# Merging three attention groups beside a triangular inverse instead of in the last stage

## The chip, the cores and the metric

The kernel runs on one core of one Trainium2 chip. The metric is the device time of one execution in microseconds (us); before the change the median of three runs is 2359.2 us. The engines are named PE (TensorE, matrix products), DVE (VectorE), ACT (ScalarE), POOL (GpSimd) and SP (SyncE, which only issues DMA transfers). Each engine works through its own instructions in a fixed order; an instruction that waits holds up all that stand behind it on that engine.

## What is computed

One decoder layer over 2048 tokens of width 1024, in float32. A normalised input is projected once; from the result two mixers run in parallel: a chunked gated delta rule (4 heads) and a dilated sliding-window attention in three groups (window 128, 512, 2048; dilation 1, 4, 16), each with 4 heads of 128. Both are gated, projected back, merged and added to the input. Cut to what matters here:

```python
tmat = triangular_solve(eye + lower, eye)           # per head and chunk of 64 tokens, 128 of them
...                                                 # the scan over chunks uses tmat
outs, lses = [], []
for gi, (window, dilation) in enumerate(SWA_GROUPS):
    o_g, lse_g = dilated_window_attention(sq[:, :, gi], sk[:, :, gi], sv[:, :, gi], window, dilation)
    outs.append(o_g); lses.append(lse_g)
alpha = softmax(stack(lses, axis=0), axis=0)        # over the three groups
o_swa = sum(alpha[..., None] * stack(outs, axis=0), axis=0)
o_swa = o_swa * silu(swa_z)
y_swa = o_swa.reshape(B, T, SWA_WIDTH) @ w_branch_swa
...
x = x + (sigmoid(g_dn) * y_dn + sigmoid(g_swa) * y_swa) @ w_out
```

The change concerns the two lines with `alpha`, here called the merge.

## The kernel before

PE does every matrix product as three products of a high and a low part of each operand, to keep float32 precision. The program is written as a sequence of PE work with hooks: after every six large matmuls `hook` advances a counter called a tick and runs whatever was put off to that tick with `at(delay, fn)`. So the order of instructions on each engine follows from ticks. From the opening of the inverse on, the order is not pinned: a planner places each instruction as early as its inputs, its buffers and its engine allow by the planner's own times, the earlier in the program first. That is why loads often stand far ahead of their place in the program.

The stages, with the times of the profile:

1. Up to about 1000 us: input projections for the attention and, between them, the attention itself. Each attention block writes its unnormalised output (128 columns), its negated maximum and its denominator (columns 128 and 129) to a DRAM buffer `oscr` of shape [T, 3 groups, 4 heads, 130].
2. `cunits` (PE matmuls at lines 720 to 722): 36 units of four blocks, 24 matmuls of 128x512 to a block, four ticks to a block. PE's results go through three PSUM banks. The units produce the delta rule's inputs (to about 1415 us), then the gates z (`z_block`, ACT and DVE, lines 1148 and 1149) and g (`g_block`, ACT only, line 1155). Each unit's weights are loaded by SP (line 697) and split into a high part by ACT (line 87) and a low part by POOL (line 88).
3. Beside the gate units, from 1415 us: `inverse`. Z with the 128 lower triangles is loaded (2 MB, line 1003), then 63 rows follow one another on DVE: a product of i x i elements (line 1020), two memsets (1021, 1022) and a reduction (1023). Row i+1 is put off by as many ticks as the row should take. After the last row the result is stored to `vscr` and, transposed by ACT and DVE (lines 1014, 1015), to `tscr`.
4. Still beside the gate units: `scan`, 16 steps. Its loads come first (lines 1042 to 1048); its first matmul (line 1058) is put off by 26 ticks from the end of the inverse. Its results go to the DRAM buffer `odn`.
5. `start_fin`, still beside the gate units: `o_load` for the first two tiles of 128 tokens, and 12 ticks later `o_start`, which transposes the four heads of `odn` and of the merge on PE (line 1221), multiplies with z (DVE, line 1222) and splits (ACT line 1225, POOL line 1226).
6. The final stage: for each of eight blocks of 256 tokens, eight `fin_y` (branch products at lines 1237 to 1239; DVE 1241, POOL 1243, ACT 1244, POOL 1245) and four `fin_out` (products with w_out at 1254 to 1256). In the first block the weights w_out are still being loaded and split (lines 1175, 1182, 1184). Between them the next two tiles' `o_load` and `o_start`.

`o_load(t)` loads `odn` for tile t (line 1212) and calls `combine(t)`, the merge: a load of 780 KB from `oscr` (line 1189), the minimum of the negated maxima (1194), the differences and their exponentials (1195, 1196 on ACT), the weights by the denominators (1197 to 1200), three products of 128x512 (1203) and two sums (1205, 1206). All but the exponential is on DVE. The buffer `oc` of the load exists once, the result `osw` twice.

Of the kernel before, what the change touches and what calls it, by code (L numbers as in the profile page):

```python
# [47 lines left out]
class Net:  # L48
# [7 lines left out]
    def setup(self):  # L56
        tc, nc, ctx, i = self.tc, self.nc, self.ctx, self.i
        self.cp = cp = ctx.enter_context(tc.tile_pool(name="const", bufs=1))
        hp = ctx.enter_context(tc.tile_pool(name="hp", bufs=1))
        self.hh = hp.tile([P, NB, KT, 512], F32R, name="hh")  # L60
        self.hl = hp.tile([P, NB, KT, 512], F32R, name="hl")
        self.hhf = self.hh.bitcast(F32)
        self.ident = cp.tile([P, P], F32, name="ident")
        self.mhalf = cp.tile([P, 8], F32, name="mhalf")
        nc.vector.memset(self.mhalf, -0.5)
        self.ab = cp.tile([P, 8, 16], F32, name="ab")
        self.step = 0
        self.tick = 0
        self.ev = []
        self.gcscr = self.scratch("gcscr", [2 * H * T])  # L70
        self.nbscr = self.scratch("nbscr", [H * T])
        self.rec = self.scratch("rec", [16, P, H, RECW])
        self.lscr = self.scratch("lscr", [H * 32, 64, 64])
        self.vscr = self.scratch("vscr", [H * 32, 64, 64])
        self.tscr = self.scratch("tscr", [H * 32, 64, 64])
        self.odn = self.scratch("odn", [T, H * P])
        self.zscr = self.scratch("zscr", [8, P, T])
        self.gscr = self.scratch("gscr", [16, P, T])
        self.qks = [[self.scratch(f"qks{h}{g}", [T, 256]) for g in range(G)] for h in range(H)]
        self.vs = [self.scratch(f"vs{g}", [T, 512]) for g in range(G)]  # L80
        self.opd = {(p, op, x): self.scratch(f"opd{p}{op}{x}", [P, 4, 512])
                    for p, op in ((0, "A11"), (0, "A12"), (0, "A21"), (0, "A22"), (1, "A21")) for x in range(2)}
        self.wdr = [[self.scratch(f"wdr{j}{x}", [P, 1024]) for x in range(2)] for j in range(56)]
        self.oscr = self.scratch("oscr", [T, G, H, 130])

    def split(self, raw, h, l, eng):
        self.nc.scalar.activation(h, raw, AF.Copy)  # L87
# [1090 lines left out]
    def w_split(self, which, k0, m, raw):  # L1178
# [4 lines left out]
        eng = nc.gpsimd if (k0 and m % 2) else nc.vector  # L1183
        eng.tensor_tensor(out=lv, in0=raw, in1=hv.bitcast(F32), op=ALU.subtract)

    def combine(self, t):
        nc, fp, V = self.nc, self.fp, self.nc.vector
        oc = fp.tile([P, G, H, 130], F32, name="oc", bufs=1)
        nc.sync.dma_start(oc.rearrange("p g h c -> p (g h c)"), dr(self.oscr, t * P * G * H * 130, [[G * H * 130, P], [1, G * H * 130]]))
        sm = fp.tile([P, 4, 12], F32, name="cs", bufs=1)  # L1190
        nm, ls = oc[:, :, :, 128], oc[:, :, :, 129]
        mn, e, c, r = sm[:, 0, 0:4], sm[:, 1, :].rearrange("p (g h) -> p g h", h=H), \
            sm[:, 2, :].rearrange("p (g h) -> p g h", h=H), sm[:, 3, 0:4]
        V.tensor_reduce(out=mn.unsqueeze(2), in_=nm.rearrange("p g h -> p h g"), axis=mybir.AxisListType.X, op=ALU.min)
        V.tensor_tensor(out=e, in0=mn.unsqueeze(1).to_broadcast([P, G, H]), in1=nm, op=ALU.subtract)
        nc.scalar.activation(e, e, AF.Exp)
        V.tensor_tensor(out=c, in0=e, in1=ls, op=ALU.mult)
        V.tensor_reduce(out=r.unsqueeze(2), in_=c.rearrange("p g h -> p h g"), axis=mybir.AxisListType.X, op=ALU.add)
        V.reciprocal(r, r)
        V.tensor_tensor(out=c, in0=e, in1=r.unsqueeze(1).to_broadcast([P, G, H]), op=ALU.mult)  # L1200
        o = fp.tile([P, H, P], F32, name="osw", bufs=2)
        for g in range(G):
            V.tensor_tensor(out=oc[:, g, :, 0:P], in0=oc[:, g, :, 0:P], in1=c[:, g, :].unsqueeze(2).to_broadcast([P, H, P]),
                            op=ALU.mult)
        V.tensor_tensor(out=o, in0=oc[:, 0, :, 0:P], in1=oc[:, 1, :, 0:P], op=ALU.add)
        V.tensor_tensor(out=o, in0=o, in1=oc[:, 2, :, 0:P], op=ALU.add)
        return o

    def o_load(self, t, x):
        nc, fp = self.nc, self.fp  # L1210
        od = fp.tile([P, H, P], F32, name="od", bufs=2)
        nc.sync.dma_start(od.rearrange("p h c -> p (h c)"), dr(self.odn, t * P * 512, [[512, P], [1, 512]]))
        x[t] = (od, self.combine(t))

    def o_prep(self, t, b, x, oh, ol):
        nc, fp = self.nc, self.fp
# [55 lines left out]
    def run(self):  # L1272
# [50 lines left out]
        pst = ExitStack()  # L1323
        self.ps = self.ctx.enter_context(tc.tile_pool(name="ps", bufs=2, space=PSUM, **tile_))
        self.scb = 2
        cst, smst, dst, ist, qst, fst = (ExitStack() for _ in range(6))
        self.rawp = self.ctx.enter_context(tc.tile_pool(name="rawp", bufs=3, **tile_))
        sm = pool(cst, "sm")
        self.gp = pool(cst, "gp")
# [16 lines left out]
        def start_inverse():  # L1346
            self.nb_out()
            pin.close()
            dst.close()
            self.inverse(pool(ist, "ip", "right"), start_scan)  # L1350

        def start_scan():
# [30 lines left out]
        du = [partial(f, h) for h in range(H) for f in (self.k_block, self.q_block, self.v_block)]  # L1383
        self.cunits(zu[:3] + du + zu[3:] + gu, {3: open_dn, 15: lambda: self.at(9, start_inverse)}, tail)
        self.flush()
        cst.close()
        self.lp = pool(fst, "lp")
        oh, ol = xo["o0"]
# [59 lines left out]
```

## Time and profile before

| | |
|---|---|
| median of three runs | 2359.2 us (2356.81 to 2360.14) |
| profiled execution | 2357.82 us |
| its span, first to last instruction | 2356.0 us |
| mean granted TensorE clock | 0.99 |
| DMA | 263.45 MB read, 185.89 MB written |

A page of the profile gives the busy time of each engine and its share of the span. The view by stage gives, for stretches of time, how long each engine was busy; the view of waits says who waited for whom, with the total, the number of times and the longest, in us; the timeline lists single instructions with start, duration, engine, line, operation, output and inputs, and in brackets the idle time of the engine just before and what ended it. "x3" behind a row are three instructions merged into one. The groups list gives count, total busy time, and mean in ns. The list of DMA issues gives size and the time from issue to landing.

### The profile page before, as it was taken

The numbers are of one execution on the slowest core, as the hardware profiler recorded it, in microseconds if no ns is written. First come the engines' busy times: TensorE is split into PE (matmuls) and PEld (weight loads), VectorE is DVE, ScalarE is ACT, GpSimd is POOL, SyncE is SP. The second block draws the span as 40 slices with busy tenths as digits, with TensorE's granted clock in tenths as the row PEclk, the third lists the DMA queues.
The fourth block names the chain that finished last, engine by engine and source line by source line (L and its number), as shares of the span: only waits on it lengthen the run. The fifth ranks groups of instructions, "written<-read, shape, count | busy, mean of one in ns | idle before, by whom it ended". The sixth has DMA issues, their size and how long they took to land.

```text
span 2356.0 us, 43344 instructions
## 1 busy us (share of the span) xinstructions
PE 2297.1 (97%) x15216; PEld 2086.2 (89%) x15216; DVE 1347.7 (57%) x2853; ACT 907.2 (39%) x2948; POOL 889.2 (38%) x1331
## 2 busy tenths in 40 slices
PE   7999999979999999999999999999999999999999
PEld 7999999879999999888787888888888788889988
DVE  6566576594435535445777767999244423444431
ACT  5345466653324435445666651111233214111110
POOL 5374266574403303402675561111232213433442
PEclk8999999999999999999999999999999999999999
DMA  9989889857887888853544443222677636554542
GB/s 296 325 277 323 272 283 292 269 161 239 251 265 236 246 273 261 259 148 101 130 110 132 127 103 113 72 76 69 212 207 208 193 120 175 161 179 150 148 139 77
DMA packets 525969, 452.23 MB, mean 192 GB/s; under 512 B 66168, under 2 KB 490424, under 8 KB 523320
## 3 DMA queue, kind: packets, MB, share of 16 engines
q1 hardware_dynamic: 525464, 449.39, 62.6%
q8 instruction: 121, 1.98, 0.3%
q14 instruction: 96, 0.79, 0.1%
q10 hardware_dynamic: 288, 0.07, 0.0%
HBM read 263.45 MB, written 185.89 MB: 191 GB/s over the span
## 4 chain that ended last, share of the span: by engine, by line
PE 66%; DMA 5%; DVE 3%; POOL 1%; ACT 1%; issue 1%; SPq 0%; DVEq 0%; POOLq 0%; ACTq 0%
PE mm L433 12%; PE mm L720 10%; PE mm L721 10%; PE mm L722 10%; PE mm L1254 2%; PE mm L1256 2%; PE mm L1255 2%; PE mm L1237 2%; PE mm L1239 2%; PE mm L1238 2%; DMA oscr<-ol 2%; DMA gcb<-gcscr 1%; PE tp L584 1%; PE po L626 1%; DMA raw<-in_w_out_dram 1%; PE tp L617 1%
## 5 line engine op out<-in xcount | busy, mean ns | idle before, releaser
L720 PE MATMUL mm<-hh,w 128*128 128x512 f32 x1152 | 463.3, 402 | 0.0
L722 PE MATMUL mm<-hh,w 128*128 128x512 f32 x1152 | 457.8, 397 | 0.0
L721 PE MATMUL mm<-hl,w 128*128 128x512 f32 x1152 | 456.9, 397 | 0.0
L433 PE MATMUL mm<-w,hh 128*128 128x256 f32 x1760 | 328.3, 286 | 0.0
L433 PEld LDWEIGHTS mm<-w,hh 128*128 128x128 f32 x1760 | 271.2, 190 | 0.0
L88 POOL TENSOR_TENSOR w<-raw,w 128x512 fp32r<-128x512 f32 x68 | 100.0, 1472 | 435.0 <-ACT w L87 434.8
L720 PEld LDWEIGHTS mm<-hh,w 128*128 128x128 f32 x1152 | 220.3, 191 | 45.9
L722 PEld LDWEIGHTS mm<-hh,w 128*128 128x128 f32 x1152 | 217.0, 188 | 46.9
L433 PE MATMUL mm<-hh 128*128 128x256 f32 x880 | 257.5, 293 | 0.0
L721 PEld LDWEIGHTS mm<-hl,w 128*128 128x128 f32 x1152 | 217.6, 189 | 42.4
L433 PE MATMUL mm<-hl,hh 128*128 128x256 f32 x880 | 249.8, 284 | 0.9 <-POOL hl L295 0.9
L433 PE MATMUL mm<-hh,hl 128*128 128x256 f32 x880 | 249.6, 284 | 0.0
L433 PE MATMUL mm<-w,hl 128*128 128x256 f32 x880 | 248.3, 282 | 0.0
L607 DVE CUSTOM_DVE_ANT_0 p<-sc,mask 128x128 f32<-128x128 f32 (+1 forms) x192 | 70.0, 365 | 213.8 <-PE sc L604 87.0
L433 PEld LDWEIGHTS mm<-hl,hh 128*128 128x128 f32 x880 | 169.4, 192 | 1.3 <-POOL hl L295 1.3
L433 PEld LDWEIGHTS mm<-hh 128*128 128x128 f32 x880 | 169.3, 192 | 0.0
L433 PEld LDWEIGHTS mm<-hh,hl 128*128 128x128 f32 x880 | 169.0, 192 | 0.0
L433 PEld LDWEIGHTS mm<-w,hl 128*128 128x128 f32 x880 | 166.1, 189 | 0.0
L368 POOL TENSOR_SCALAR st<-st 128x4 f32<-128x4 f32 x96 | 21.1, 219 | 374.0 <-ACT junk L367 371.9
L1237 PE MATMUL mm<-oh,hh 128*128 128x256 f32 x512 | 143.7, 281 | 1.7 <-DVE gt L1241 1.7
L1239 PE MATMUL mm<-oh,hl 128*128 128x256 f32 x512 | 142.9, 279 | 0.0
L1238 PE MATMUL mm<-ol,hh 128*128 128x256 f32 x512 | 142.9, 279 | 0.0
(304 smaller groups left out, 5492.1 us busy)
## 6 DMA issues: line engine op xcount, KB each, us to landing
wdr<-w SPq DMA_DIRECT2D x56, 512.0 KB, 4.8
w<-wdr SPq DMA_DIRECT2D x54, 512.0 KB, 5.1
qk<-qks SPq DMA_DIRECT2D x212, 128.0 KB, 3.9
qks<-rec SPq DMA_DIRECT2D x96, 256.0 KB, 3.2
raw<-in_w_in_dram SPq DMA_DIRECT2D x68, 256.0 KB, 3.3
gscr<-gt SPq DMA_DIRECT2D x64, 256.0 KB, 2.5
gt<-gscr SPq DMA_DIRECT2D x64, 256.0 KB, 3.4
wdr<-hh SPq DMA_DIRECT2D x28, 512.0 KB, 4.4
```

The costliest lines, as they stand in the source:

```text
L88: eng.tensor_tensor(out=l, in0=raw, in1=h.bitcast(F32), op=ALU.subtract)
L433: mm = lambda x, y, **kw: nc.tensor.matmul(o, x, y, skip_group_check=True, **kw)
L607: nc.vector.tensor_tensor_reduce(out=p[:, lo:hi], in0=sc[:, lo:hi], in1=self.mask[:, slot * P + lo:slot * P + hi], scalar=3e38, scale=-SCA ...
L720: nc.tensor.matmul(pr, wh[:, k, :], a, start=(k == 0), stop=False)
L721: nc.tensor.matmul(pr, wh[:, k, :], b, start=False, stop=False)
L722: nc.tensor.matmul(pr, wl[:, k, :], a, start=False, stop=(k == KT - 1))
L1237: nc.tensor.matmul(o, self.wbh[:, k, ms], oh[:, k, :], start=(k == b * 4), stop=False)
L1238: nc.tensor.matmul(o, self.wbh[:, k, ms], ol[:, k, :], start=False, stop=False)
L1239: nc.tensor.matmul(o, self.wbl[:, k, ms], oh[:, k, :], start=False, stop=(k == b * 4 + 3))
L1254: nc.tensor.matmul(pr, mh[:, k, cs], self.woh[:, k, hs], start=(k == 0), stop=False)
L1255: nc.tensor.matmul(pr, mh[:, k, cs], self.wol[:, k, hs], start=False, stop=False)
L1256: nc.tensor.matmul(pr, ml[:, k, cs], self.woh[:, k, hs], start=False, stop=(k == KT - 1))
```

## The change

The merge leaves the final stage. At the start of the inverse a pool `cb` is opened and `comb_setup` loads the first tile; from eight ticks later on a tile is merged every nine ticks, with the steps put off to ticks 1 to 6. Both buffers that a tile needs (`oc`, `cs`) exist twice, and the next tile's load is issued at the start of a tile. The minimum stays on DVE. The differences, the weights and the two sums go to POOL; there the reciprocal is a power with exponent -1 (a tensor of -1 as second input) and the sum over groups is two additions. The three products of 128x512 become twelve scalings of 128x128 on ACT, one for each group and head, with the weight as the scale. The result is written into group 0's part of `oc` and stored to a new DRAM buffer `osd` (256 KB a tile). `o_load` in the final stage only loads it. The pool is closed before the final stage.

```diff
+        self.osd = self.scratch("osd", [T, H * P])
...
+    def comb_setup(self, cb):
+        self.cb = cb
+        self.mone = cb.tile([P, 4], F32, name="mone", bufs=1)
+        self.nc.gpsimd.memset(self.mone, -1.0)
+        self.comb_load(0)
+        self.at(8, lambda: self.combine(0))
+
+    def comb_load(self, t):
+        oc = self.oc = self.cb.tile([P, G, H, 130], F32, name="oc", bufs=2)
+        self.nc.sync.dma_start(oc.rearrange("p g h c -> p (g h c)"),
+                               dr(self.oscr, t * P * G * H * 130, [[G * H * 130, P], [1, G * H * 130]]))
+
     def combine(self, t):
-        nc, fp, V = self.nc, self.fp, self.nc.vector
-        oc = fp.tile([P, G, H, 130], F32, name="oc", bufs=1)
-        nc.sync.dma_start(oc.rearrange("p g h c -> p (g h c)"), dr(self.oscr, t * P * G * H * 130, [[G * H * 130, P], [1, G * H * 130]]))
-        sm = fp.tile([P, 4, 12], F32, name="cs", bufs=1)
+        nc, cb, V = self.nc, self.cb, self.nc.gpsimd
+        oc = self.oc
+        if t < 15:
+            self.comb_load(t + 1)
+        sm = cb.tile([P, 4, 12], F32, name="cs", bufs=2)
...
-        V.tensor_reduce(out=mn.unsqueeze(2), in_=nm.rearrange("p g h -> p h g"), axis=mybir.AxisListType.X, op=ALU.min)
+        nc.vector.tensor_reduce(out=mn.unsqueeze(2), in_=nm.rearrange("p g h -> p h g"), axis=mybir.AxisListType.X, op=ALU.min)
         V.tensor_tensor(out=e, in0=mn.unsqueeze(1).to_broadcast([P, G, H]), in1=nm, op=ALU.subtract)
-        nc.scalar.activation(e, e, AF.Exp)
-        V.tensor_tensor(out=c, in0=e, in1=ls, op=ALU.mult)
-        V.tensor_reduce(out=r.unsqueeze(2), in_=c.rearrange("p g h -> p h g"), axis=mybir.AxisListType.X, op=ALU.add)
-        V.reciprocal(r, r)
-        V.tensor_tensor(out=c, in0=e, in1=r.unsqueeze(1).to_broadcast([P, G, H]), op=ALU.mult)
-        o = fp.tile([P, H, P], F32, name="osw", bufs=2)
+
+        def share():
+            nc.scalar.activation(e, e, AF.Exp)
+            V.tensor_tensor(out=c, in0=e, in1=ls, op=ALU.mult)
+            V.tensor_tensor(out=r, in0=c[:, 0], in1=c[:, 1], op=ALU.add)
+            V.tensor_tensor(out=r, in0=r, in1=c[:, 2], op=ALU.add)
+            V.tensor_tensor(out=r, in0=r, in1=self.mone, op=ALU.pow)
+            V.tensor_tensor(out=c, in0=e, in1=r.unsqueeze(1).to_broadcast([P, G, H]), op=ALU.mult)
+
+        def weigh(g):
+            for h in range(H):
+                nc.scalar.activation(oc[:, g, h, 0:P], oc[:, g, h, 0:P], AF.Identity, scale=c[:, g, h:h + 1])
+
+        def add(g):
+            o = oc[:, 0, :, 0:P]
+            V.tensor_tensor(out=o, in0=o, in1=oc[:, g, :, 0:P], op=ALU.add)
+            if g == 2:
+                nc.sync.dma_start(dr(self.osd, t * P * 512, [[512, P], [P, H], [1, P]]), o)
+        self.at(1, share)
         for g in range(G):
-            V.tensor_tensor(out=oc[:, g, :, 0:P], in0=oc[:, g, :, 0:P], in1=c[:, g, :].unsqueeze(2).to_broadcast([P, H, P]),
-                            op=ALU.mult)
-        V.tensor_tensor(out=o, in0=oc[:, 0, :, 0:P], in1=oc[:, 1, :, 0:P], op=ALU.add)
-        V.tensor_tensor(out=o, in0=o, in1=oc[:, 2, :, 0:P], op=ALU.add)
-        return o
+            self.at(3 + g, lambda g=g: weigh(g))
+        for g in (1, 2):
+            self.at(4 + g, lambda g=g: add(g))
+        if t < 15:
+            self.at(9, lambda: self.combine(t + 1))
...
     def o_load(self, t, x):
...
-        x[t] = (od, self.combine(t))
+        os = fp.tile([P, H, P], F32, name="osw", bufs=2)
+        nc.sync.dma_start(os.rearrange("p h c -> p (h c)"), dr(self.osd, t * P * 512, [[512, P], [1, 512]]))
+        x[t] = (od, os)
...
             dst.close()
+            self.comb_setup(pool(bst, "cb"))
             self.inverse(pool(ist, "ip", "right"), start_scan)
...
         self.flush()
+        bst.close()
         cst.close()
```

More of the change, by code (lines that the diff above doesn't have):

```diff
@@ L1325, in run @@
         self.scb = 2
-        cst, smst, dst, ist, qst, fst = (ExitStack() for _ in range(6))
+        cst, bst, dst, ist, qst, fst = (ExitStack() for _ in range(6))
         self.rawp = self.ctx.enter_context(tc.tile_pool(name="rawp", bufs=3, **tile_))
```

## The prediction

> **What bounds the kernel now.** I read the page's busy times first, then the busy time of each engine by stage, then who makes TensorE (PE) wait from 1395 us on, the part of the program that the change can touch.
>
> ```profile
> PE 2297.1 (97%) x15216; PEld 2086.2 (89%) x15216; DVE 1347.7 (57%) x2853; ACT 907.2 (39%) x2948; POOL 889.2 (38%) x1331
> ```
>
> ```profile
> 1415.00:1655.00 240.00, 240.00 (x1041) 196.35 (x1040) 220.53 (x276) 38.67 (x66) 40.05 (x23) 1.00 0.27 84
> 1655.00:1870.00 215.00, 215.00 (x1400) 186.42 (x1399) 77.73 (x250) 75.36 (x273) 59.41 (x176) 1.00 0.68 201
> 1870.00:2356.00 486.00, 474.40 (x2857) 420.49 (x2855) 185.00 (x321) 81.71 (x167) 157.97 (x174) 0.99 0.49 148
> ```
>
> ```profile
> PE tp L1221 <- DVE osw L1206: 3.9, 1, 3.9
> PE mm L1254 <- ACT mh L1244: 2.2, 3, 1.0
> PE mm L1237 <- DVE gt L1241: 1.7, 2, 1.4
> ```
>
> The columns of a stage are its length, then PE, weight loads, VectorE (DVE), ScalarE (ACT), GpSimd (POOL), granted clock, DMA share and GB/s. PE is busy 97% of the span. The inverse (1415 to 1655) and the scan (1655 to 1870) leave it no idle time at all, so work that goes away on another engine is worth only what PE waits for it. The merge runs on DVE in the last stage, where DVE has 301 of 486 us free. PE waits for it once, 3.9 us; the other two waits concern the final matmuls' evictions.
>
> This is that one wait on PE, beside an undisturbed set of the same four transposes:
>
> ```profile
> 1877.33 0.60 PE L1221 MATMUL tp<-ident,od 128*128 128x128 f32 x4
> ...
> 1884.62 1.09 PE L1221 MATMUL tp<-ident,osw 128*128 128x128 f32 x4 [3.91 <-DVE osw L1206]
> 1885.36 0.78 PE L720 MATMUL mm<-hh,w 128*128 128x512 f32 x1
> ...
> 1889.74 0.39 PE L721 MATMUL mm<-hl,w 128*128 128x512 f32 x1
> 1889.97 0.39 PE L722 MATMUL mm<-hh,w 128*128 128x512 f32 x1
> ```
>
> The wait costs more than its 3.9 us. At its usual pace PE starts a 128x512 matmul every 0.23 us (1889.74 to 1889.97). Right after the wait the ten from 1885.36 up to 1889.74 took 4.38 us instead of 2.3, and the four transposes 1.09 us instead of 0.60. PE runs at about half pace for some 4 us after it stood idle. Price: 3.9 + 2.1 + 0.5 = **6.5 us**.
>
> On DVE the cause is the merge of the second token tile:
>
> ```profile
> 1877.05 0.17 DVE L1194 TENSOR_REDUCE cs<-oc 128x4 f32<-128x12 f32 x1 [3.39 <-DMA oc<-oscr]
> ...
> 1879.09 4.05 DVE L1203 TENSOR_TENSOR oc<-oc,cs 128x512 f32<-128x512 f32 x3
> 1883.07 0.68 DVE L1205 TENSOR_TENSOR osw<-oc 128x512 f32<-128x512 f32 x1
> 1883.78 0.69 DVE L1206 TENSOR_TENSOR osw<-osw,oc 128x512 f32<-128x512 f32 x1
> ```
>
> It waits for its 780 KB load, then takes from 1877.05 to 1884.47.
>
> **Removed from the final stage.** All sixteen merges leave DVE and the last stage. Fifteen hid under PE and are worth nothing; the one in front of PE is worth 6.5 us. The new load of the merged tile is 256 KB, the size of the odn load beside it, which lands in 4.1 us, and both tiles' loads can go at the stage's start:
>
> ```profile
> oc<-oscr SPq DMA_DIRECT2D x1, 780.0 KB
> od<-odn SPq DMA_DIRECT2D x2, 256.0 KB, 4.1
> ```
>
> What is late next there is the z product of the same transposes; it too sat on DVE behind the reduce that waited 3.39 us for the load, so it comes earlier. I count the whole 6.5 us. The other two waits (2.2 and 1.7 us) lie in the first final block and hang on the splitting of w_out; no merge is behind them, and I leave them.
>
> **Added beside the inverse: ScalarE.** Per tile 12 scalings of 128x128 and one small exponential. Four such scalings take 1.14 us here, so 12 take 3.4 us, 55 us for sixteen tiles, on an engine that is busy 38.67 of 240 us.
>
> ```profile
> 1787.38 1.14 ACT L1087 ACTIVATE qs<-sc,egc 128x128 f32<-128x128 f32 x4 [3.43 <-DVE rr L1084]
> ```
>
> ```profile
> 1786.03 0.20 POOL L1116 TENSOR_TENSOR oss<-oss,cq 128x2 f32<-128x2 f32 x1
> ```
>
> An eviction of PE's PSUM bank can queue behind four scalings (1.1 us). There are three banks, each filled for 24 x 0.23 = 5.5 us, so about two fills, 11 us, hide it. Cost nothing; without that cover it would be 1.1 us a tile.
>
> **Added: GpSimd, and through it VectorE.** Per tile GpSimd gets two adds of 128x512, five small operations (about 0.20 us each, the last row above) and one power. The inverse is a chain of 63 rows on DVE, each a product (L1020) and a reduction, and DVE is 92% busy (220.53 of 240 us). What GpSimd does to it shows in these rows, of DVE, of GpSimd and of the two groups from 1437 to 1655:
>
> ```profile
> 1437.74 0.16 DVE L1020 TENSOR_TENSOR Z<-M 128x1 f32<-128x1 f32 x1
> ...
> 1468.11 1.48 DVE L1020 TENSOR_TENSOR Z<-M 128x784 f32<-128x784 f32 x1
> ...
> 1636.89 4.16 DVE L1020 TENSOR_TENSOR Z<-M 128x3844 f32<-128x3844 f32 x1
> ```
>
> ```profile
> 1467.47 1.29 POOL L88 TENSOR_TENSOR w<-raw,w 128x512 fp32r<-128x512 f32 x1 [18.05 <-ACT w L87]
> ```
>
> ```profile
> L1020 DVE TENSOR_TENSOR Z<-M 128x1 f32<-128x1 f32 (+62 forms) x63 | 103.9, 1649 | 2.9
> ```
>
> ```profile
> L88 POOL TENSOR_TENSOR w<-raw,w 128x512 fp32r<-128x512 f32 x20 | 36.6, 1836 | 187.7 <-ACT w L87 187.7
> ```
>
> The products with 1 and 3844 elements give 0.16 us plus 1.04 ns an element. By that the one with 784 should take 0.97 us; it took 1.48, because GpSimd's split ran until 1468.76: the two exclude each other. Over all 63 rows (85,344 elements) the line gives 63 x 0.16 + 88.8 = 98.9 us; the group took 103.9. So 20 splits of 1.29 us (25.8 us of GpSimd) cost DVE 5.0 us, 0.25 us each or 0.19 us per us.
>
> - 32 adds, like the splits in size: 32 x 0.25 = 8.0 us; between 0 and 32 x 0.51 = 16.3 (each as bad as the row above).
> - 80 small operations, 16 us of GpSimd: up to 3.0 us by the same rate; I take 0.8, as most follow the new reduce closely, when DVE is at a reduction of its own.
> - 16 reduces on DVE at 0.17 us: 2.7 us at most, 0 if all fall into gaps between dependent operations; I take 1.4.
> - 16 powers: nothing, by these two rows, GpSimd's power and three DVE operations with both inputs in SBUF:
>
> ```profile
> 1187.51 1.04 POOL L903 TENSOR_TENSOR ss<-ss,mhalf 128x4 f32<-128x4 f32 x1
> ```
>
> ```profile
> 1187.80 2.36 DVE L834 SCALAR_TENSOR_TENSOR acc<-xr,cw,acc 128x512 f32<-128x512 f32 x3
> ```
>
> Had the three waited for the power's end at 1188.55, they would have had 1.61 us left, 0.54 each, less than the 0.69 that the line above gives for 512 elements. So they ran beside it.
>
> The Trainium skill (SBUF — State Buffer, "Who interferes with whom") speaks against this change: a DVE tensor_tensor with both inputs in SBUF and a GpSimd operation that reads SBUF lock each other out for the whole instruction, whichever came first, while a tensor_reduce never contends. The split above agrees with it, the power does not; by the rule the powers would count too (a rival, below).
>
> - Two 780 KB loads go out around the inverse's own 2 MB load, which landed in 9.0 us:
>
> ```profile
> Z<-lscr SPq DMA_DIRECT2D x1, 2048.0 KB, 9.0
> ```
>
> Sharing the bandwidth with one of them costs up to 780/2048 x 9.0 = 3.4 us; the first can go while that load still waits for another, so 0 at best. I take 1.0.
>
> Sum: the inverse ends 8.0 + 0.8 + 1.4 + 1.0 = **11.2 us** later, between 0 and 25.4 (16.3 + 3.0 + 2.7 + 3.4).
>
> **How much of that PE sees.** The scan's first matmul (L1058) stands at a fixed place in PE's order and needs a load that waits for the inverse's stored result:
>
> ```profile
> 1667.00:1668.00 1.00, 1.00 (x6) 0.83 (x5) 0.00 (x0) 0.08 (x1) 0.85 (x1) 1.00 0.00 0
> ```
>
> ```profile
> 1668.47 0.38 SPq L697 DMA_DIRECT2D raw<-in_w_in_dram  x1
> ...
> 1670.23 0.62 SPq L1044 DMA_DIRECT2D lo<-rec  x1
> ```
>
> ```profile
> lo<-rec SPq DMA_DIRECT2D x1, 64.0 KB, 7.8
> ```
>
> ```profile
> L1058 PE MATMUL sc<-t,lo x128: 218/218/267, 1685.9 to 1841.2; 64*64 64x64 f32 x128
> ```
>
> The load issued at 1670.23 landed 7.8 us later, at 1678.0; L1058 ran at 1685.9: 7.9 us to spare. Besides, DMA was empty from 1667.0 on, so the result was stored by then, and the scan's loads stood in SP's queue behind a weight load (L697) until 1668.47: another 1.5 us. Slack 9.4 us. A delay of 11.2 leaves 1.8 us of waiting, and I take so short a wait to cost no pace. One of 3.9 us or more I price with the 2.6 us (2.1 + 0.5) at half pace.
>
> The queues that the moved steps join: SP gets 16 loads and 16 stores there; a store waits for the last add, and the gate stores and weight loads queue behind it for the length of an add, 1.29 us, under the same 11 us of PSUM cover. On GpSimd a weight split (L88) can stand behind a merge operation that waits for DVE; it has a whole unit, 4 x 5.5 = 22 us, before PE needs it. A tile goes every nine hooks of six matmuls, 9 x 6 x 0.23 = 12.4 us, so sixteen end some 200 us after 1415, before the inverse does. DVE's reduce waits for its tile's load, with the rows behind it; but the load goes out a tile, 12.4 us, ahead, against the 9.0 us of a 2 MB one. ScalarE's exponential waits for GpSimd's difference and that for the reduce; if DVE runs 11.2 us late, the evictions behind the exponential use up that same PSUM cover.
>
> **Sum.** 6.5 us won, 1.8 us given back: 4.7 us less. The profiled execution took 2357.82 us, 1.82 us around its span, and would come to 2353.1; it lies 1.4 us under the median of 2359.2, on which the forecast stands: **2354.5 us**. That is 0.2%, about what a measurement of this kernel can tell from no change.
>
> **Rivals.**
> - *Slower: GpSimd locks the inverse.* Sign turns where the new wait and its half pace cost 6.5 us: 3.9 + 2.6, a delay of 13.3 us; over 0.2% slower from 4.7 more, a delay of 18.0 us. With the upper bounds it is 25.4 us: 16.0 of waiting + 2.6 - 6.5 = 12.1 us slower, 2371.3. For it: DVE has 8% free there. Against: the measured rate gives 8.0 us for the adds, and long reductions late in the inverse leave GpSimd room. Chance 0.23.
> - *No change.* The delay lies between 11.2 and 18.0 us; at 14 us it is 4.6 + 2.6 - 6.5, 0.7 us slower, 2359.9. Chance 0.18.
> - *The powers lock DVE as well.* Then 16 x 1.04 us of GpSimd at 0.19 add 3.2 us: a delay of 14.4 us, 5.0 + 2.6 - 6.5 = 1.1 us slower, 2360.3, no change either. Against: the two rows above; a power is mostly computing. Chance 0.07. It is what the rule of the Trainium skill says.
> - *The change does not do what it says.* Another load or the z product takes the place of the merged tile in front of the transposes, and about 2359.2 stays. Against: both are on SP's and DVE's queues before it and get earlier. Chance 0.06.
> - *More is won.* The first final block's waits (3.9 us together, its half pace beside) go as well because the DMA queues are emptier: 2354.5 - 3.9 = 2350.6 or less. Against: the merge's DVE work is not in front of them. Chance 0.06.
>
> **How the numbers follow.** The forecast, a delay of at most 11.2 us, has 0.40, its own span 2352.7 (nothing given back) to 2354.5. With "more is won" faster comes to 0.46; no change has 0.18 + 0.07 + 0.06 = 0.31, slower 0.23. The range, 2350.5 to 2365, leaves out most of the last rival and the worse part of the first, a delay over some 19 us.
>
> **What would show it.** Right: L1221 is gone from PE's waits and the granted clock is full around 1880; L1020's group grows from 103.9 by 8 to 10 us; the last reduction ends some 11 us later against PE's order; PE waits 0 to 2 us at L1058. Wrong: a wait of over 4 us at L1058, matmuls at 0.43 us behind it; GpSimd's adds far over 1.3 us; or the transposes still waiting, now for a load.

## The result, and the profile after

The change makes the kernel slower: 2411.1 us (median of four runs, 2409.0 to 2412.9) against 2358.0 beside it, a ratio of 1.0224 with a 95% interval of 1.0206 to 1.0242, 53.1 us. The forecast was 2354.5 us and the range ended at 2365.0. The profiled execution took 2410.51 us, its span 2408.7. Lines 1020 and 1058 of before are 1021 and 1059 here; line 1221 and those behind it in the final stage are 29 further down.

The busy times in the page of after:

```profile
PE 2312.0 (96%) x15216; PEld 2092.1 (87%) x15216; DVE 1276.7 (53%) x2693; ACT 956.2 (40%) x3140; POOL 964.0 (40%) x1460
```

DVE lost 71 us of work and ACT and POOL gained 49 and 75, as the change says; none of the three is near full. So first: from which point does PE run late? The first scan matmul of after, and one transpose ahead of the inverse, before and after:

```profile
L1059 PE MATMUL sc<-t,lo x128: 218/218/267, 1743.5 to 1898.8; 64*64 64x64 f32 x128
```

```profile
L992 PE MATMUL tp<-ident,nbr x1: 270/270/270, 1415.3 to 1415.3; 128*64 128x128 f32 x1
```

```profile
L993 PE MATMUL tp<-ident,nbr x1: 270/270/270, 1472.9 to 1472.9; 128*64 128x128 f32 x1
```

The scan starts 57.6 us late (1685.9 before), and the transpose ahead of the inverse is 57.6 us late already. From that transpose to the scan it is 270.6 us in both kernels: nothing is lost beside the inverse, all of it is lost earlier. (How late is good to some 7 us: in `late_o` and `late_o32` below, which are as before up to there, the transpose stands at 1408.5 and 1414.4 us.) Then the first matmul of the final stage, after:

```profile
L1266 PE MATMUL mm<-oh,hh x512: 278/280/393, 2027.3 to 2382.7; 128*128 128x256 f32 x171
```

It stood at 1976.2 before, so it is 51.1 us late: 6.5 us have been won back between scan and final stage (283.8 us instead of 290.3), the very sum that the prediction had for the wait at the transposes. At the span's end the kernel is 52.7 us late. From 1860 us on PE waits only for these two:

```profile
PE mm L1266 <- DVE gt L1270: 2.3, 1, 2.3
PE mm L1283 <- ACT mh L1273: 2.0, 3, 0.8
```

What happens ahead of 1473 us? The merge does. Its sixteen loads, and its scalings and additions in the groups of after:

```profile
L1196 SPq DMA_DIRECT2D oc<-oscr x16: 319/352/538, 1018.8 to 1220.7; - x16
```

```profile
L1221 ACT ACTIVATE oc<-oc,cs 128x128 f32<-128x128 f32 x192 | 64.5, 397 | 60.5 <-POOL cs L1217 58.3 <-DMA osd<-oc 2.3
L1225 POOL TENSOR_TENSOR oc<-oc 128x512 f32<-128x512 f32 x32 | 44.3, 1386 | 36.2 <-ACT oc L1221 33.7 <-ACT cs L1212 2.2
```

The loads go out from 1018.8 to 1220.7 us. The merge does not run beside the inverse (from 1473 us on here) but among the last attention blocks and the delta rule's preparation, where the planner put it: the attention's results are there, the buffers are free, and ticks mean nothing to it. The stretch from 1000 to 1250 us, before and after:

```profile
1000.00:1250.00 250.00, 246.12 (x1271) 203.07 (x1270) 162.93 (x331) 136.68 (x440) 107.64 (x139) 0.99 0.48 126
```

```profile
1000.00:1250.00 250.00, 203.62 (x956) 162.07 (x955) 128.87 (x275) 149.59 (x519) 142.91 (x210) 0.92 0.58 164
```

PE is busy 42.5 us less, and the granted clock of 0.92 instead of 0.99 is worth about 17.5 us of the 250. Together 60.0, a rough estimate that lies close to the 57.6 above: this stretch holds the loss. ACT is busy 13 us more of 250, POOL 35 us. What PE waits for there (after, 940 to 1480 us, the five longest; all rows of this view add up to 52.5 us in after and 10.8 in before):

```profile
PE sc L603 <- ACT kq L592: 11.0, 6, 3.4
PE sc L945 <- POOL kql L931: 8.4, 5, 3.9
PE tp L983 <- ACT sq L948: 6.7, 1, 6.7
PE tp L891 <- DVE kT L840: 6.2, 5, 2.2
PE tp L891 <- DVE xr L823: 5.3, 1, 5.3
```

None of these tiles belongs to the merge. They are the attention's and the delta rule's own evictions and splits, now late. All engines' waits, 1000 to 1400 us, after:

```profile
ACT oc L1221 <- POOL cs L1217: 58.3, 15, 11.3
POOL cs L1209 <- DVE cs L1208: 37.0, 5, 26.6
...
POOL oc L1225 <- ACT oc L1221: 33.7, 13, 4.1
...
ACT cs L1212 <- POOL cs L1209: 19.4, 8, 7.2
```

These belong to the merge: its engines wait for one another, at the head of queues that hold PE's work behind them. One case in the timeline of after, ACT, then POOL, DVE and PE:

```profile
1133.46 0.28 ACT L1212 ACTIVATE cs<-cs 128x12 f32<-128x12 f32 x1
1133.67 0.37 ACT L896 ACTIVATE st<-tp,ek 128x128 f32<-128x128 f32 x1
1141.65 1.28 ACT L1221 ACTIVATE oc<-oc,cs 128x128 f32<-128x128 f32 x4 [7.61 <-POOL cs L1217]
```

```profile
1135.73 1.75 POOL L1225 TENSOR_TENSOR oc<-oc 128x512 f32<-128x512 f32 x1
1137.44 0.67 POOL L903 TENSOR_SCALAR ss<-ss 128x4 f32<-128x4 f32 x1
1138.19 1.04 POOL L904 TENSOR_TENSOR ss<-ss,mhalf 128x4 f32<-128x4 f32 x1
1139.20 0.22 POOL L1213 TENSOR_TENSOR cs<-cs,oc 128x12 f32<-128x12 f32 x1
...
1140.19 1.04 POOL L1216 TENSOR_TENSOR cs<-cs,mone 128x4 f32<-128x4 f32 x1
1141.21 0.23 POOL L908 TENSOR_SCALAR nbr<-ss 128x4 f32<-128x4 f32 x1
1141.41 0.21 POOL L1217 TENSOR_TENSOR cs<-cs 128x12 f32<-128x12 f32 x1
```

```profile
1145.07 0.69 DVE L840 SCALAR_TENSOR_TENSOR kT<-kT,acc 128x512 f32<-128x512 f32 x1 [6.00 <-ACT kT L839]
```

```profile
1145.82 0.69 PE L891 MATMUL tp<-ident,kT 128*128 128x128 f32 x2 [5.34 <-DVE xr L823]
```

ACT's exponential is done at 1133.74. POOL's first step on it starts only at 1139.20, behind an addition of the tile before and the delta rule's own small steps, and the weights are out at 1141.62. All that time ACT stands in front of its scalings. The eviction kT (line 839) is queued behind them, DVE waits 6.00 us for it, and PE 5.34 us for DVE. Behind the stop PE starts a matmul every 0.43 us (1146.73, 1147.16, 1147.59); ahead of it, it was 0.23 (1139.62, 1139.85). POOL is slow here, too: the addition at 1135.73 takes 1.75 us beside DVE operations with both inputs in SBUF (line 835, 4.17 us for three), where the shortest of the 32 takes 1.28.

### The profile page after: what moved, and what is told of

It is laid out like the page before. It is cut to its first block, busy times and chain, and to the rows that moved or that the text cites. A ratio compares the mean times of both kernels' runs of the same rounds, so it can differ in the third digit from the quotient of the medians.

```text
span 2408.7 us, 43608 instructions
## 1 busy us (share of the span) xinstructions
PE 2312.0 (96%) x15216; PEld 2092.1 (87%) x15216; DVE 1276.7 (53%) x2693; ACT 956.2 (40%) x3140; POOL 964.0 (40%) x1460
## 4 chain that ended last, share of the span: by engine, by line
PE 61%; DMA 5%; POOL 5%; ACT 4%; DVE 2%; issue 1%; SPq 0%; POOLq 0%; DVEq 0%; ACTq 0%
PE mm L434 12%; PE mm L721 8%; PE mm L722 8%; PE mm L723 8%; PE mm L1283 2%; PE mm L1285 2%; PE mm L1284 2%; PE mm L1266 2%; PE mm L1268 2%; PE mm L1267 2%; ACT oc L1221 1%; DMA oscr<-ol 1%; PE tp L585 1%; DMA gcb<-gcscr 1%; POOL oc L1225 1%
```

## The experiments

The theory that grew from this: a chain over four engines, each working in order, costs PE the time that ACT and POOL stand at the head of their queues. The rivals: the place; GpSimd's lock against DVE; ACT's and POOL's work as such. Where a text below says "before", it is the kernel before, measured beside the experiment on the same chip. Some of these kernels leave out a part of the merge or its weights, so that their results are not the merged values: they are there to be timed.

**The place.** `held` writes one element of the first two tiles' buffers from a tile that the inverse loads, so that the planner cannot start earlier (`comb_setup` is called at the end of the inverse's own setup for that):

```diff
+        self.comb_setup(nb)
...
         oc = self.oc = self.cb.tile([P, G, H, 130], F32, name="oc", bufs=2)
+        if t < 2:
+            self.nc.gpsimd.tensor_copy(oc[:, 0, 0, 0:1], self.nb[:, 0:1])
```

> The merge is the same, but its first two loads must wait for a value that exists only once the delta rule's stage is over, so the planner can no longer place it there and it has to run beside the inverse. If the place is what costs the time, the prediction's own working holds here: the inverse ends about 11 us later, PE waits 0 to 4 us at the scan's first matmul, and the time is 2352 to 2360 us. If the merge costs PE as much wherever it stands, the time stays over 2390 us.

Measured: 2400.6 us (before 2355.6), ratio 1.0194 [1.0176, 1.0212]. The loads now go out from 1417.6 to 1581.3, beside the inverse, and 45.0 of the 53 us are still lost. The place is not the cause by itself. From the transpose ahead of the inverse to the scan, PE now takes 324.4 us for the matmuls that took 270.6. The longest of all waits from 1430 to 1605 us:

```profile
ACT oc L1225 <- POOL cs L1221: 54.0, 16, 5.5
ACT cs L1216 <- POOL cs L1213: 42.0, 14, 5.8
...
PE mm L721 <- DVE gt L1152: 26.2, 9, 6.0
...
PE mm L721 <- ACT gt L1158: 11.5, 3, 5.8
```

The chain is the same, and the victims here are the gate evictions: PE waits 37.7 us for them, none of it before. The cover of 11 us by three PSUM banks does not hold, although no single wait on ACT is longer than 5.8 us. One case, ACT and PE in `held`:

```profile
1499.70 0.21 ACT L1216 ACTIVATE cs<-cs 128x12 f32<-128x12 f32 x1 [2.86 <-POOL cs L1213]
1502.19 0.99 ACT L1225 ACTIVATE oc<-oc,cs 128x128 f32<-128x128 f32 x3 [2.28 <-POOL cs L1221]
1503.08 0.58 ACT L1151 ACTIVATE gt<-mm 128x512 f32<-128x512 f32 x1
```

```profile
1504.43 0.50 PE L721 MATMUL mm<-hh,w 128*128 128x512 f32 x1 [3.21 <-DVE gt L1152]
```

The gate eviction at 1503.08 stands behind the scalings of one tile, then two waits and three scalings of the next; the one before it had run at 1493.92. DVE's half of the eviction (line 1152) waits for it, and PE for DVE.

**The scalings: their work or their wait.** `free_scale` keeps the 192 scalings but gives them a constant, so they no longer wait for the weights; `no_scale` leaves them out (the groups are summed unweighted):

```diff
-                nc.scalar.activation(oc[:, g, h, 0:P], oc[:, g, h, 0:P], AF.Identity, scale=c[:, g, h:h + 1])
+                nc.scalar.activation(oc[:, g, h, 0:P], oc[:, g, h, 0:P], AF.Identity, scale=self.mone[:, 0:1])
```

```diff
-            self.at(3 + g, lambda g=g: weigh(g))
+            pass
```

> The changed kernel, with the twelve scalings of a tile taking a constant as scale in place of GpSimd's weights, so the merged values are not the weighted ones. ScalarE has as much work as before, but no scaling waits for GpSimd. If ScalarE's queue standing behind those waits (58.3 us in the trace) is what holds PE up, most of the 53 us go: under 2375 us. If it is the added busy time, the time stays within 15 us of 2411 us.

> The changed kernel without the 192 scalings, so the sums are of unweighted values; GpSimd's work, the loads and the stores stay. If ScalarE, by waiting or by work, is what holds PE up, the time is under 2370 us. If GpSimd's operations and their lock with VectorE hold up the delta rule's stage, it stays over 2390 us.

Measured: 2380.3 us, 1.0106 [1.0089, 1.0123], and 2383.6 us, 1.0127 [1.0109, 1.0146]. Taking away the scalings' wait alone gives 28 us back, about half, somewhat less than the theory's figure (under 2375 us). Taking away the 64.5 us of work as well gives nothing more, and 2383.6 lies between both figures expected. That does not show that the work is free, for a wait came in its place: the exponential waits 62.1 us for POOL's difference in `no_scale`, 17.9 in `free_scale` (940 to 1480 us). Waiting for GpSimd is what these two runs show to cost time.

**What the rest is made of.** `dma_only` keeps loads and stores alone, `adds_only` those and the two additions:

```diff
-        nc.vector.tensor_reduce(out=mn.unsqueeze(2), in_=nm.rearrange("p g h -> p h g"), axis=mybir.AxisListType.X, op=ALU.min)
-        V.tensor_tensor(out=e, in0=mn.unsqueeze(1).to_broadcast([P, G, H]), in1=nm, op=ALU.subtract)
...
-        self.at(1, share)
...
-            self.at(3 + g, lambda g=g: weigh(g))
+            pass
```

`dma_only` also leaves out this line:

```diff
-            V.tensor_tensor(out=o, in0=o, in1=oc[:, g, :, 0:P], op=ALU.add)
```

> The kernel after the change with the loads and stores of the merge alone and no arithmetic (group 0 is copied through). Both theories: the 6.5 us at the final stage's first transposes are won and nothing is paid, 2349 to 2353 us. If the 16.6 MB of transfers in the stage from 1000 us on are what costs, 2360 us or more.

> The kernel after the change with the loads, GpSimd's two additions and the stores, but without the minimum, the weights and the scalings (the three groups are summed unweighted). Theory (a chain over four engines on queues that work in order): one engine and no chain, so 2350 to 2358 us, the 6.5 us of the last stage won. Rival (the additions of 1.3 us shut out VectorE): most of the 25 us that stayed without scalings stay, 2370 to 2380 us.

Measured (before 2354.1): 2350.7 us, 0.9987 [0.9977, 0.9997], and 2364.8 us, 1.0048 [1.0033, 1.0064]. The transfers cost next to nothing: with them alone the kernel is faster by 3.4 us between the medians (0.7 to 5.4 by the interval), inside the 2349 to 2353 us expected, PE waits 14.1 us from 940 to 1480 instead of 10.8, and the transpose ahead of the inverse stands at 1411.2 us, within the 1408.5 to 1415.3 of the kernels without the transfers. The additions cost 14.0 us more: too much for the theory in the form it had then, under the rival's number too. It takes no chain of four engines. POOL in `adds_only` (here the additions are line 1223):

```profile
1130.76 1.37 POOL L1223 TENSOR_TENSOR oc<-oc 128x512 f32<-128x512 f32 x1 [2.15 <-DMA oc<-oscr]
...
1136.35 3.42 POOL L1223 TENSOR_TENSOR oc<-oc 128x512 f32<-128x512 f32 x2
1139.72 1.18 POOL L931 TENSOR_TENSOR kql<-kT,kqh 128x256 fp32r<-128x256 f32 x1
```

The split kql, for which PE waits 9.9 us in this kernel, stands behind 3.42 us of additions, and other work behind an addition that waits for its load (41.1 us in sum). Those two additions are stretched as well (the shortest takes 1.27 us), beside DVE operations of line 835 in SBUF. How much of the 14 us comes by the queue and how much by the lock, no run separates.

**GpSimd's small operations on DVE, where the planner put the merge.** `small_dve` changes the change in one thing:

```diff
-        V.tensor_tensor(out=e, in0=mn.unsqueeze(1).to_broadcast([P, G, H]), in1=nm, op=ALU.subtract)
+        nc.vector.tensor_tensor(out=e, in0=mn.unsqueeze(1).to_broadcast([P, G, H]), in1=nm, op=ALU.subtract)
...
-            V.tensor_tensor(out=c, in0=e, in1=ls, op=ALU.mult)
-            V.tensor_tensor(out=r, in0=c[:, 0], in1=c[:, 1], op=ALU.add)
-            V.tensor_tensor(out=r, in0=r, in1=c[:, 2], op=ALU.add)
-            V.tensor_tensor(out=r, in0=r, in1=self.mone, op=ALU.pow)
-            V.tensor_tensor(out=c, in0=e, in1=r.unsqueeze(1).to_broadcast([P, G, H]), op=ALU.mult)
+            W = nc.vector
...
+            W.tensor_tensor(out=c, in0=e, in1=ls, op=ALU.mult)
+            W.tensor_reduce(out=r.unsqueeze(2), in_=c.rearrange("p g h -> p h g"), axis=mybir.AxisListType.X, op=ALU.add)
+            W.reciprocal(r, r)
+            W.tensor_tensor(out=c, in0=e, in1=r.unsqueeze(1).to_broadcast([P, G, H]), op=ALU.mult)
```

> The kernel after the change, order by the planner, with the difference and the weights' small operations on VectorE; scalings stay on ACT, additions on GpSimd. The planner will put the merge in the stage from 1000 us again. Theory: the chain loses two of its three passages to GpSimd, but ACT still waits at the head of its queue, now for VectorE: 2365 to 2390 us, faster than after (2411) by 20 us or more. Rival (the place decides, that stage has no room for scalings and additions at all): 2395 us or more.

Measured: 2381.2 us (before 2354.6), 1.0114 [1.0099, 1.0129]. Half of the loss goes, as the theory expected and as much as with `free_scale`, and ACT waits 7.5 us for the weights instead of 58.3. Three ways to take GpSimd out from in front of ACT's scalings end within 3.5 us of each other.

Side by side, PE's waits from 940 to 1480 us and the time against before:

| kernel | PE waits, us | time, us |
|---|---|---|
| before | 10.8 | 0 |
| dma_only | 14.1 | -3.4 |
| adds_only | 25.2 | +10.6 |
| free_scale | 32.6 | +24.8 |
| small_dve | 33.3 | +26.6 |
| no_scale | 33.7 | +28.1 |
| after | 52.5 | +53.1 |

With the 6.5 us won in the final stage added to the time, each us of waiting above before's costs 1.2 us in `adds_only` and 1.4 to 1.5 us in the four below it: (53.1 + 6.5) / (52.5 - 10.8) = 1.43 in after. Pace after each stop, as the prediction had it at line 1221 and as the case above shows it, accounts for at least a part of the difference; no run separates the rest.

**The order.** Is it the planner's packing? `pin_after` gives PE, ACT, DVE and POOL the written order from the opening of the inverse to the scan, `pin_before` does the same to the kernel before:

```diff
...
+            pinv.enter_context(pinned(False))
             self.inverse(pool(ist, "ip", "right"), start_scan)
...
         def start_scan():
+            pinv.close()
```

> The kernel after the change, all steps kept, but from the opening of the inverse to the start of the scan the order on PE, ACT, DVE and POOL is the written one (each step at the tick that the program gives it) and not the planner's. The merge then stands beside the inverse, a tile every nine ticks, its steps one to two ticks (1.4 to 2.8 us) apart. Theory (the loss comes from steps packed so closely by the planner that each waits for the other engine at the head of its queue): nearly all of the 53 us goes, 2350 to 2365 us if the written order costs nothing by itself. Rival (GpSimd's operations shutting out VectorE, and the sheer work added): as slow as with the merge held beside the inverse, 2395 to 2405 us.

> Control for the run above: the kernel before, with the same stretch in the written order. Both theories: 2355 to 2362 us; whatever it differs from the kernel before is the price of the written order alone and is taken off the run above.

Measured: 2396.6 us, 1.0183 [1.0168, 1.0198]; control 2364.5 us, 1.0047 [1.0032, 1.0062]. The written order costs 10 us by itself, more than the 2355 to 2362 us expected, and the merge 32.1 us on top. My theory of the planner's packing fell: with steps one to two ticks apart the time lies where the rival had it (2395 to 2405 us), 4 us under `held`.

**Steps drawn apart.** `pin_spread` puts the difference four ticks behind the minimum, the exponential two behind that, and so on, with three buffers for `oc` and `cs`; the first tile starts four ticks later, the next tile's load goes out at tick 3, the store follows two ticks behind the last addition, and the written order starts ten ticks later. `pin10_before` is its control:

```diff
-        V.tensor_tensor(out=e, in0=mn.unsqueeze(1).to_broadcast([P, G, H]), in1=nm, op=ALU.subtract)
+        self.at(4, lambda: V.tensor_tensor(out=e, in0=mn.unsqueeze(1).to_broadcast([P, G, H]), in1=nm, op=ALU.subtract))
...
-            nc.scalar.activation(e, e, AF.Exp)
...
-        self.at(1, share)
+        self.at(6, lambda: nc.scalar.activation(e, e, AF.Exp))
+        self.at(8, share)
-            self.at(3 + g, lambda g=g: weigh(g))
+            self.at(11 + g, lambda g=g: weigh(g))
-            self.at(4 + g, lambda g=g: add(g))
+            self.at(12 + 2 * g, lambda g=g: add(g))
```

```diff
+            self.at(10, lambda: pinv.enter_context(pinned(False)))
             self.inverse(pool(ist, "ip", "right"), start_scan)
```

> The kernel after the change with every instruction of the merge kept on its engine, in the written order from ten ticks after the opening of the inverse to the start of the scan, and with the steps drawn apart: minimum at tick 0, difference at 4, exponential at 6, weights at 8, scalings at 11 to 13, additions at 14 and 16, store at 18, three buffers for the load. Theory (PE loses the time that ACT and GpSimd stand at the head of their queues waiting for the engine before them in the chain): the waits of ACT for GpSimd fall from 150 us (with the written order and steps one to two ticks apart) to under 40, and at least two thirds of the 32 us over the control go: within 11 us of the control. Rival (GpSimd and VectorE shutting each other out, and the work as such): still 25 to 35 us over the control, since every operation is still there at the same place.

> Control for the run above: the kernel before with the written order from ten ticks after the opening of the inverse to the start of the scan. Both theories: within 12 us of the kernel before; less than with the whole inverse in the written order (2364.5 us, 10 us over), if the first rows of the inverse are what that order costs.

Measured: 2385.2 us, 1.0124 [1.0110, 1.0138]; control 2363.5 us, 1.0035 [1.0022, 1.0049]. One third of the 32 us goes, where two thirds were expected; ACT's waits for GpSimd fall from 154.6 us (110.0 for the difference, 44.6 for the weights) to 83.1, not under 40. One reason why so much is left is seen on POOL and DVE of `pin_spread`:

```profile
1539.39 2.32 POOL L1212 TENSOR_TENSOR cs<-cs,oc 128x12 f32<-128x12 f32 x1
1541.79 0.20 POOL L1213 TENSOR_TENSOR cs<-cs 128x4 f32<-128x4 f32 x1
...
1549.73 2.41 POOL L1209 TENSOR_TENSOR cs<-cs,oc 128x12 f32<-128x12 f32 x1 [6.08 <-DVE cs L1208]
```

```profile
1539.36 2.27 DVE L1021 TENSOR_TENSOR Z<-M 128x2025 f32<-128x2025 f32 x1
1541.71 0.11 DVE L1022 MEMSET M<- 128x64 f32 x1
1541.86 2.26 DVE L1024 TENSOR_REDUCE M<-Z 128x45 f32<-128x2025 f32 x1
...
1549.61 2.46 DVE L1021 TENSOR_TENSOR Z<-M 128x2209 f32<-128x2209 f32 x1
```

```profile
L1209 POOL TENSOR_TENSOR cs<-cs,oc x16: 212/1713/3761, 1442.7 to 1658.6; 128x12 f32<-128x12 f32 x16
```

A POOL operation on 12 elements takes as long as the DVE product beside it: 2.32 us, to the product's end, where the next, of 4 elements beside a DVE reduction, takes 0.20. Line 1209 takes 0.21 to 3.76 us, 1.71 in the median. That is the lock of the Trainium skill (SBUF — State Buffer, "Who interferes with whom"): exclusive for the whole instruction, and issue order decides who blocks. The trace agrees. I had priced it for DVE only; here GpSimd is the one shut out, and ACT, which waits for GpSimd, pays.

The power is shut out too, when the product comes first. In this case on POOL and DVE it takes 3.90 us, where most of the 16 take 1.02:

```profile
1592.32 3.90 POOL L1215 TENSOR_TENSOR cs<-cs,mone 128x4 f32<-128x4 f32 x1
```

```profile
1592.15 3.20 DVE L1021 TENSOR_TENSOR Z<-M 128x2916 f32<-128x2916 f32 x1
```

The other way round it holds up nothing: the product of 3600 elements that starts at 1636.74, half a microsecond into a power (1636.21, 1.02 us), takes 3.91 us, the 0.16 plus 1.04 ns an element of the prediction. Here the measurement differs from a lock for the whole instruction.

**Two cures for that.** `pin_small_dve` is `pin_spread` with the small operations on DVE as in `small_dve`; `pin_const` is `pin_spread` with the constant of `free_scale`.

> The run with the steps drawn apart in the written order (2385.2 us, 21 us over its control of 2363.5), but with the difference and the weights' small operations on VectorE, among the inverse's rows, as the kernel before has them in its last stage; GpSimd keeps the two additions. Theory (GpSimd's small operations of 0.2 us take up to 3.8 us there because VectorE's products shut them out, ACT waits 60 us for them with PE's evictions behind it): on VectorE they take 0.2 us each, ACT's waits for the weights fall under 15 us, and the run comes within 8 us of the control, although the inverse gets some 1 us a tile more to do. Rival (ACT's scalings and the additions as such are too much for the stage): still 18 us or more over the control.

> The same run with the steps drawn apart, small operations on GpSimd, but the scalings take a constant instead of the weights (the weights are worked out and not used): ACT keeps all its work and loses the wait for the weights. Theory: ACT's wait for the weights was most of the loss, so 10 us or more less than 2385.2, the exponential's wait of 21 us being left. Rival (GpSimd itself is late with the weight splits that PE needs): 2380 to 2386 us, nothing gained.

Measured: 2377.9 us, 1.0100 [1.0083, 1.0117], and 2379.6 us, 1.0106 [1.0091, 1.0121]. Against the control's 1.0035 that is 0.0065 and 0.0071, 15.3 and 16.7 us, where `pin_spread` has 0.0089, 21.0 us; the intervals of the three overlap. `pin_const` is 5.6 us under `pin_spread`, neither 10 nor nothing, and `pin_small_dve` falls between both theories' numbers too.

The profiles tell them apart better. From the transpose ahead of the inverse to the first scan matmul PE does the same work in each kernel (1172 or 1173 matmuls), and this stretch is the same to 0.1 us in the nine kernels that have the planner's order and no merge in it:

| kernel | stretch, us | above its control, us |
|---|---|---|
| before, after and seven more | 270.6 to 270.7 | |
| held | 324.4 | 53.8 (before) |
| pin_before | 281.4 | |
| pin_after | 317.7 | 36.3 |
| pin10_before | 283.7 | |
| pin_spread | 308.2 | 24.5 |
| pin_small_dve | 300.1 | 16.4 |
| pin_const | 299.1 | 15.4 |

Drawing the steps apart takes away one third, and each of the two cures a third of what is left. In `pin_small_dve` the wait moved to DVE (from all waits, 1400 to 1720 us):

```profile
ACT cs L1227 <- DVE cs L1209: 56.9, 15, 14.3
...
ACT oc L1220 <- DVE cs L1216: 34.8, 6, 7.8
```

On DVE the small steps stand behind rows of up to 4.64 us of product and 4.28 of reduction (lines 1021 and 1024); ACT waits for those instead, 34.8 us for the weights and 37.6 more in front of the scalings for nothing that the profile shows, not under 15. In `pin_const` the exponential still waits 41.6 us for the difference. PE's waits from 1400 to 1760 us are 32.2 us in `pin_after`, 24.7 in `pin_spread`, 20.3 in `pin_const` and 17.9 in `pin_small_dve`, against 8.5 and 9.0 in the two controls. How the last 15 us divide between ACT's waits, the additions on POOL and the weight splits behind them stays open; no run takes them apart.

**The gain without the change.** What the change wins is one wait of PE at the first transposes. `late_o` and `late_o32` leave the merge in the final stage of the kernel before and put those transposes off by 20 and 32 ticks:

```diff
-            self.at(12, lambda: xo.update(o0=self.o_start(0, xo)))
+            self.at(32, lambda: xo.update(o0=self.o_start(0, xo)))
```

> The kernel before with one number changed: the first transposes of the last stage are put off by 20 ticks in place of 12, so the merge in front of them is ready. If the one wait on PE costs 6.5 us with the half pace behind it, the time is about 2351.5 us, and the row for osw is gone from PE's waits. If the wait only moves to another input, the time stays at 2358 us; if only the 3.9 us of standing still count, it is 2354 us.

> The kernel before with the first transposes of the final stage (o_start) put off by 32 ticks instead of 12, the merge left where it was. If the wait only needs time, the wait for the merged tile and that for the z product (3.5 us with 20 ticks) are both gone: 4 to 7 us faster than before, as fast as the change's loads and stores alone. Rival: something else of the last stage then comes late in front of PE, and it gains no more than 20 ticks did, 2 to 3 us.

Measured: 2352.4 us, 0.9989 [0.9976, 1.0001], and 2349.2 us (before 2354.9), 0.9971 [0.9962, 0.9981]. PE's waits from 1800 us on, `late_o` and then `late_o32`:

```profile
PE tp L1221 <- DVE z L1222: 3.5, 1, 3.5
...
```

```profile
PE mm L1237 <- DVE gt L1241: 2.4, 4, 0.9
PE mm L1254 <- ACT mh L1244: 1.7, 2, 1.1
```

With 20 ticks the wait only changes its name, from the merged tile to the z product behind it; with 32 it is gone, and the gain of 4.5 to 8.9 us (the interval) holds the 6.5 that the wait was priced at. The profiles say it more sharply: from the first scan matmul to the first matmul of the final stage it is 290.3 us in before, 287.5 in `late_o`, and 283.8 in `late_o32`, `dma_only` and after alike. A change of one number gains all that the change was meant to win, and beats both kernels.

## Why the prediction was wrong, step by step

- **Removed from the final stage: right.** 6.5 us predicted, 6.5 us between scan and final stage in after (57.6 - 51.1), `dma_only` and `late_o32` (290.3 - 283.8). Of whole times, `late_o32` gains 4.5 to 8.9 us and `dma_only` 0.7 to 5.4. The prediction did not ask why that one merge was late: its three products took 4.05 us where the first tile's took 1.90 (1868.84), beside two GpSimd operations (1879.51 to 1882.60).
- **"A tile goes every nine hooks ... so sixteen end some 200 us after 1415, before the inverse does": the step that failed first.** The merge ran from 1018.8 us on. My own account of the kernel said that the planner places each instruction as early as inputs and buffers allow; the step went by ticks all the same. So no term of the sum spoke of the stage in which the time was lost. Getting this step right would not have saved the forecast, as `held` shows.
- **"The evictions behind the exponential use up that same PSUM cover", priced at nothing: the step that failed most.** It failed in the predicted place too: `held` loses 45.0 us, and PE waits 37.7 us there for evictions behind the merge's steps. I counted the delay of one wait, the exponential's, against one cover of 11 us, and named no wait of the scalings for the weights at all. The cover is spent by the waits in a row on one queue, with the scalings between them: two waits a tile on ACT, 96 us over sixteen tiles in `held`.
- **"Cost nothing" for ACT's scalings: wrong for the instructions, open for the work.** That each set stands in front of evictions until GpSimd has its weights costs 28 us (`free_scale`). Whether the 64.5 us of work by themselves cost nothing, no run shows, since another wait grew when they were left out (`no_scale`).
- **GpSimd's additions, 8.0 us on DVE: wrong side of the lock.** Where they really run beside the inverse, its products take 106.7 us (`held`) and 106.9 (`pin_after`) instead of 103.9: 3 us, well under the 8.0, and PE waits for the inverse at the scan's first matmul in none of the kernels. With the additions alone on GpSimd (`pin_small_dve`) they take 103.6. It is GpSimd that pays: the 32 additions take 58.5 us in `pin_after`, 1.83 each, and an operation of 0.20 us becomes 1.7 in the median in `pin_spread`. The small operations were priced at 0.8 us "as most follow the new reduce closely, when DVE is at a reduction of its own"; but that reduce stands between a row's reduction and the next row's product (1549.49, then 1549.61 in `pin_spread`), so GpSimd's difference met the product. And in the earlier stage the additions cost 14 us (`adds_only`).
- **The powers, priced at nothing: right for DVE.** A product that starts during a power is not slowed (3.91 us above). The other way round a power behind a product is shut out, 3.90 us for 1.02, and it lies on the path from the exponential to the scalings.
- **The slower rival** was GpSimd locking the inverse, at most 12.1 us. Its engine was right, its victim wrong; the delay of the inverse was never what PE saw. That it had the direction is luck. Nothing in "what would show it" looked ahead of 1415 us.

## What to carry to other kernels

An engine that is 16% busy, as ACT was beside the inverse, still is no free place for a step of a chain over several engines: ask not how long the operation takes but how long it stands at the head of its queue, and what of PE's is behind it. Before pricing work by where the program puts it, find where the planner will: at the earliest point at which its inputs and buffers exist. And when all that a change can win is one wait, first try to give that wait time.

## What the runs showed of the hardware beyond that

- GpSimd's operation of 12 elements took 0.21 us beside a DVE reduction and up to 3.76 us beside a DVE product with both inputs in SBUF (line 1209 of `pin_spread`), some eighteen times as long.
- A GpSimd power of 1.02 us became 3.90 behind a DVE product, but a DVE product that started during a power was not slowed.
- 192 scalings of 128x128 on ACT ran at 0.39 us each (`held`) and 0.30 when queued back to back (12 in 3.63 us), in step with what four took in the row of before (1.14 us).
- 16 loads of 780 KB and 16 stores of 256 KB, moved into a stage that already kept DMA 0.48 busy (the row of before from 1000 to 1250 us), cost no time that the runs can tell (`dma_only`).
